# Binary cross-entropy on one core: the last full store issued from GpSimd instead of SyncE

## The chip, the core and the metric

The kernel runs on one core of a Trainium2 chip. Its time is the device time of one execution, in microseconds (us). The core has five engines that run their own instruction streams; here VectorE (DVE), ScalarE (ACT), GpSimd (POOL) and SyncE (SP) are used. Transfers between HBM and the on-chip memory SBUF are carried by 16 DMA engines. A transfer is issued by an instruction of ScalarE, GpSimd or SyncE and goes into that engine's DMA queue: in the profile q0 is GpSimd's queue, q1 SyncE's and q10 ScalarE's.

## The reference

Both inputs and the output are 8192 x 8192 float32; target holds zeros and ones.

```python
def reference(pred, target):
    eps = 1e-7
    pred = np.clip(pred, eps, 1 - eps)
    return -(target * np.log(pred) + (1 - target) * np.log(1 - pred))
```

With target 0 or 1 this is -log|pred + target - 1|, which is how the kernel computes it.

## The kernel before

The arrays are taken as flat and cut into 39 chunks, each spread over 128 partitions. Chunk 0 is 8192 elements wide in each partition, chunks 1 to 35 are 14336 wide (7168 KB in float32, or 7.34 MB), and three tail chunks follow: 6656, 6656 and 1024 wide. The last full chunk, number 35, is called z; the tail chunks 36, 37 and 38 are called a, b and c.

Two areas of SBUF hold the data. `ring_p` has three slots of 14336 float32 columns; a full chunk takes the slots in turn, and the three tail chunks lie side by side in one slot. `ring_t` has one slot of 14336 bfloat16 columns for target; the load converts float32 to bfloat16 on the way, so a target chunk reads as many bytes from HBM as a pred chunk and writes half as many into SBUF.

For each chunk there are these steps, the loop's full chunks done in halves:

- `load_p` (L70) and `load_t` (L73): load pred and target. All are issued from GpSimd, but for pred of chunk 0, which ScalarE issues.
- `clip` (L85): VectorE limits pred to [eps, 1-eps], in place.
- `merge` (L91, L94, L95): VectorE adds target - 1, in place; then ScalarE takes the absolute value and the logarithm, in place.
- `negate` (L99): VectorE multiplies by -1, in place.
- `store` (L79): the result goes from `ring_p` to HBM.

The order of the instructions on each engine is written out by hand. A trip k of the loop (k from 0 to 34) merges chunk k, loads target of k+1, negates k, clips k+1, stores k and loads pred of k+2; in this loop every store goes through GpSimd's queue. After the loop, chunk z is merged; then GpSimd issues the loads of a, b and c (pred, then target, of each). VectorE's order from there is: negate the first half of z, clip a, negate the second half of z, merge a, clip b, merge b, negate a, clip c, merge c, negate b, negate c. The stores of z, a, b and c are issued from SyncE in this order, each when its negate is done; the store of c is cut into three pieces by rows (108, 12 and 8 partitions). Dependences between engines become semaphore waits. An engine issues in program order, so an instruction that waits holds up what is behind it on the same engine.

The list `ROWS` cuts the last store, and z in the code is the number of the last full chunk.

Of the kernel before, what the change touches and what calls it, by code (L numbers as in the profile page):

```python
# [1 line left out]

# [4 lines left out]

EPS = 1e-7

WIDE = 14336  # L10
SLOTS = 3
TAIL = (6656, 6656, 1024)
ROWS = (108, 12, 8)


@with_exitstack
def kernel(
    ctx: ExitStack,
    tc: tile.TileContext,
    pred: bass.AP,  # L20
    target: bass.AP,
    out: bass.AP,
):
    nc = tc.nc
    fp32 = mybir.dt.float32
    low = mybir.dt.bfloat16
    Alu = mybir.AluOpType
    Act = mybir.ActivationFunctionType
    P = nc.NUM_PARTITIONS

    R, C = pred.shape
    total = R * C // P
    rest = total - sum(TAIL)
    n = rest // WIDE
    first = rest - n * WIDE
    assert 0 < first <= WIDE and n > 4 and sum(TAIL) <= WIDE
    spots = [(first, 0)]
    spots += [(WIDE, k % SLOTS * WIDE) for k in range(1, n + 1)]
    c = (n + 1) % SLOTS * WIDE
    for w in TAIL:  # L40
        spots.append((w, c))
        c += w
    n = len(spots)
    z = n - 1 - len(TAIL)
    starts = [sum(w for w, _ in spots[:k]) * P for k in range(n)]

    pool = ctx.enter_context(tc.tile_pool(name="rings", bufs=1))
    ring_p = pool.tile([P, SLOTS * WIDE], fp32, name="ring_p", tag="ring_p")
    ring_t = pool.tile([P, WIDE], low, name="ring_t", tag="ring_t")
    warm = pool.tile([1, 8], fp32, name="warm", tag="warm")  # L50

    def chunk(ap, k):
        flat = ap.rearrange("r c -> (r c)")
        w = spots[k][0]
        return flat[starts[k] : starts[k] + w * P].rearrange("(p w) -> p w", p=P)

    def cols(ring, k, part, c):
        w = spots[k][0]
        i, m = part
        return ring[:, c + i * w // m : c + (i + 1) * w // m]  # L60

    def p_of(k, part=(0, 1)):
        return cols(ring_p, k, part, spots[k][1])

    def t_of(k, part=(0, 1)):
        return cols(ring_t, k, part, spots[k][1] % WIDE)

    def load_p(k):
        queue = nc.scalar if k == 0 else nc.gpsimd
        queue.dma_start(out=p_of(k), in_=chunk(pred, k))  # L70

    def load_t(k):
        nc.gpsimd.dma_start(out=t_of(k), in_=chunk(target, k))  # L73

    def store(k):
        queue = nc.sync if k >= z else nc.gpsimd
        r = 0
        for rows in ROWS if k == n - 1 else (P,):
            queue.dma_start(out=chunk(out, k)[r : r + rows, :], in_=p_of(k)[r : r + rows, :])  # L79
            r += rows  # L80
        assert r == P

    def clip(k, *part):
        p = p_of(k, *part)
        nc.vector.tensor_scalar(  # L85
            out=p, in0=p, scalar1=EPS, scalar2=1 - EPS, op0=Alu.max, op1=Alu.min
        )

    def merge(k, *part):
        p, t = p_of(k, *part), t_of(k, *part)  # L90
        nc.vector.scalar_tensor_tensor(  # L91
            out=p, in0=t, scalar=1.0, in1=p, op0=Alu.subtract, op1=Alu.add
        )
        nc.scalar.activation(out=p, in_=p, func=Act.Abs)  # L94
        nc.scalar.activation(out=p, in_=p, func=Act.Ln)  # L95

    def negate(k, *part):
        p = p_of(k, *part)
        nc.vector.tensor_scalar(out=p, in0=p, scalar1=-1.0, scalar2=None, op0=Alu.mult)  # L99

    halves = (0, 2), (1, 2)
    with tc.manual_schedule():
        load_p(0)
        load_t(0)
        load_p(1)
        nc.vector.memset(warm, 1.0)  # L106
        nc.scalar.activation(out=warm, in_=warm, func=Act.Ln)  # L107
        for h in halves:
            clip(0, h)
        for k in range(z):  # L110
            for h in halves:
                merge(k, h)
            load_t(k + 1)
            for h in halves:
                negate(k, h)
            for h in halves:
                clip(k + 1, h)
            store(k)
            if k + 2 <= z:
                load_p(k + 2)  # L120
        for h in halves:
            merge(z, h)
        a, b, c = range(z + 1, n)
        for j in a, b, c:
            load_p(j)
            load_t(j)
        negate(z, halves[0])
        clip(a)
        negate(z, halves[1])
        store(z)  # L130
        merge(a)
        clip(b)
        merge(b)
        negate(a)
        store(a)
        clip(c)
        merge(c)
        negate(b)
        store(b)
        negate(c)  # L140
        store(c)


# [1 line left out]
_INS = ['pred', 'target']  # L145
_OUTS = [((8192, 8192), 'float32')]


# [23 lines left out]
```

## Time and profile before

| | |
|---|---|
| median of 3 runs | 1882.25 us (1881.54 to 1882.39) |
| the profiled execution, its own time | 1880.78 us |
| its span in the profile | 1879.0 us |
| VectorE busy | 1118.3 us, 60% of the span |
| ScalarE busy | 901.7 us, 48% |
| GpSimd busy | 282.8 us, 15% |
| read from HBM, written to HBM | 536.87 MB, 268.44 MB |
| rate counted so | 429 GB/s over the span |
| through GpSimd's queue | 652.22 MB as the DMA rows count them |
| through SyncE's queue | 14.68 MB |

The DMA rows of the profile count a transfer by one side, so a target load counts with its smaller bfloat16 size there; the HBM counts show what was read. A transfer's row gives its size and the time from issue to landing, which includes the time in which it stood in its queue behind others. A DMA share of 1 in a stretch of time means that all 16 DMA engines were busy in it. In a timeline row the first figure is the start, counted from the span's start, and the second the length; the brackets say how long the engine had stood idle before it, and what ended that. "SPq" and "POOLq" mean an instruction that issues a transfer on that engine.

### The profile page before, as it was taken

How to read it: one execution, taken by the hardware profiler on the slowest of the kernel's cores; microseconds unless marked ns; L12 is line 12 of the kernel's file. 1: busy time of each engine (PE TensorE's matmuls, PEld its weight loads, DVE VectorE, ACT ScalarE, POOL GpSimd, SP SyncE). 2: the span in 40 equal slices, each digit the busy share in tenths (PEclk: the TensorE clock that was granted, in tenths of full speed). 3: DMA queues.
4: the chain of work that ended last, by engine and by line, in shares of the span. 5: the costliest groups of instructions: out<-in, count | busy, mean ns of one | idle time of the engine just before them, and what ended most of it. 6: DMA issues, size and time to landing. Idle time of an engine off the chain costs nothing.

```text
span 1879.0 us, 697 instructions
## 1 busy us (share of the span) xinstructions
DVE 1118.3 (60%) x226; ACT 901.7 (48%) x152; POOL 282.8 (15%) x116
## 2 busy tenths in 40 slices
DVE  4675566565555665556656555566555666665563
ACT  3555444444455555554444444555555444444473
POOL 0121111111111110111111111111101111111100
DMA  9999999999999999999999999999999999999996
GB/s 329 338 375 372 370 352 366 355 352 352 359 359 355 355 371 376 374 373 359 359 358 358 352 353 361 358 354 364 375 374 374 369 353 363 355 354 354 359 363 239
DMA packets 16869, 671.14 MB, mean 357 GB/s; under 512 B 1888, under 2 KB 1888, under 8 KB 2272
## 3 DMA queue, kind: packets, MB, share of 16 engines
q0 software_dynamic: 16128, 652.22, 97.0%
q1 hardware_dynamic: 592, 14.68, 1.8%
q10 hardware_dynamic: 144, 4.19, 0.6%
q14 instruction: 5, 0.04, 0.0%
HBM read 536.87 MB, written 268.44 MB: 429 GB/s over the span
## 4 chain that ended last, share of the span: by engine, by line
DMA 64%; issue 28%; ACT 3%; DVE 2%; another core or an unknown queue 1%; POOL 0%; POOLq 0%; DVEq 0%; PEldq 0%
DMA ring_t<-in_target_dram 64%; ACT ring_p L95 2%; ACT ring_p L94 2%; DVE ring_p L91 2%; DVE ring_p L99 0%; POOL out_dram L79 0%; DVE ring_p L85 0%; POOL ring_p L70 0%; DVEq L167 0%; POOLq L73 0%; POOLq L79 0%; DVEq L91 0%; PEldq L167 0%
## 5 line engine op out<-in xcount | busy, mean ns | idle before, releaser
L94 ACT ACTIVATE ring_p<-ring_p 128x7168 f32<-128x7168 f32 (+3 forms) x75 | 451.6, 6021 | 959.1 <-DVE ring_p L91 959.1
L91 DVE SCALAR_TENSOR_TENSOR ring_p<-ring_t,ring_p 128x7168 f32<-128x7168 bf16 (+3 forms) x75 | 554.8, 7437 | 252.2 <-DMA ring_t<-in_target_dram 252.2
L99 DVE TENSOR_SCALAR ring_p<-ring_p 128x7168 f32<-128x7168 f32 (+3 forms) x75 | 285.0, 3802 | 475.0 <-ACT ring_p L95 475.0
L95 ACT ACTIVATE ring_p<-ring_p 128x7168 f32<-128x7168 f32 (+3 forms) x75 | 452.1, 6029 | 2.4
L85 DVE TENSOR_SCALAR ring_p<-ring_p 128x7168 f32<-128x7168 f32 (+3 forms) x75 | 281.9, 3799 | 20.3 <-DMA ring_p<-in_pred_dram 20.3
L79 POOL DMA_DIRECT2D out_dram<-ring_p x35 | 126.9, 3625 | 710.8 <-DVE ring_p L99 710.8
L73 POOL DMA_DIRECT2D ring_t<-in_target_dram x39 | 20.7, 532 | 801.1 <-DVE ring_p L91 800.3
L70 POOL DMA_DIRECT2D ring_p<-in_pred_dram x38 | 135.3, 3561 | 0.0
L107 ACT ACT_TABLE_LOAD x1 | 1.3, 1283 | 1.1 <-PEq L156 1.1
L106 DVE MEMSET warm<- 1x8 f32 x1 | 0.1, 65 | 0.8 <-PEq L156 0.8
L107 ACT ACTIVATE warm<-warm 1x8 f32<-1x8 f32 x1 | 0.2, 208 | 0.0
L156 POOL MEMSET const-float32-0.0<- 128x1 f32 x1 | 0.1, 100 | 0.2 <-issue 0.2
L156 POOL MEMSET const-bfloat16-1.0<- 128x1 bf16 x1 | 0.1, 102 | 0.0
L156 POOL MEMSET const-float32-1.0<- 128x1 f32 x1 | 0.1, 100 | 0.0
L156 POOL MEMSET const-uint8-127<- 128x1 uint8 x1 | 0.1, 99 | 0.0
## 6 DMA issues: line engine op xcount, KB each, us to landing
ring_p<-in_pred_dram POOLq DMA_DIRECT2D x35, 7168.0 KB, 44.4
out_dram<-ring_p POOLq DMA_DIRECT2D x34, 7168.0 KB, 31.0
ring_t<-in_target_dram POOLq DMA_DIRECT2D x35, 3584.0 KB, 35.2
out_dram<-ring_p SPq DMA_DIRECT2D x1, 7168.0 KB, 28.9
ring_p<-in_pred_dram POOLq DMA_DIRECT2D x2, 3328.0 KB, 34.7
out_dram<-ring_p SPq DMA_DIRECT2D x2, 3328.0 KB, 9.6
ring_p<-in_pred_dram ACTq DMA_DIRECT2D x1, 4096.0 KB, 19.6
out_dram<-ring_p POOLq DMA_DIRECT2D x1, 4096.0 KB, 21.2
```

The lines of the kernel that those rows point to most:

```text
L70: queue.dma_start(out=p_of(k), in_=chunk(pred, k))
L73: nc.gpsimd.dma_start(out=t_of(k), in_=chunk(target, k))
L79: queue.dma_start(out=chunk(out, k)[r : r + rows, :], in_=p_of(k)[r : r + rows, :])
L85: nc.vector.tensor_scalar(out=p, in0=p, scalar1=EPS, scalar2=1 - EPS, op0=Alu.max, op1=Alu.min)
L91: nc.vector.scalar_tensor_tensor(out=p, in0=t, scalar=1.0, in1=p, op0=Alu.subtract, op1=Alu.add)
L94: nc.scalar.activation(out=p, in_=p, func=Act.Abs)
L95: nc.scalar.activation(out=p, in_=p, func=Act.Ln)
L99: nc.vector.tensor_scalar(out=p, in0=p, scalar1=-1.0, scalar2=None, op0=Alu.mult)
L106: nc.vector.memset(warm, 1.0)
L107: nc.scalar.activation(out=warm, in_=warm, func=Act.Ln)
L156: nc = _bacc.Bacc("TRN2", target_bir_lowering=False, num_devices=1)
```

## The change

The store of chunk z, 128 x 14336 float32, is issued from GpSimd instead of SyncE. On GpSimd it stands behind the last loads (pred and target of a, b and c), as the last transfer that this engine issues. The stores of a, b and c stay on SyncE. Nothing else is changed: the same bytes are moved, and the other engines' instructions are the same in the same order.

```diff
     def store(k):
-        queue = nc.sync if k >= z else nc.gpsimd
+        queue = nc.sync if k > z else nc.gpsimd
         r = 0
         for rows in ROWS if k == n - 1 else (P,):
             queue.dma_start(out=chunk(out, k)[r : r + rows, :], in_=p_of(k)[r : r + rows, :])
```

## The prediction

> Below, z is the last full chunk and a, b, c are the three tail chunks; p, t and s stand for a chunk's load of pred, its load of target and its store. "s_z" is the store that moves. A change of 0.2%, 3.8 us here, is about the least that a measurement of this kernel can tell from none.
>
> **What bounds the kernel now.** I read the page's DMA row first, then the rows of every engine in the tail, then each tail transfer's row, then the DMA share in stretches of 2 us. On the page:
>
> ```profile
> DVE 1118.3 (60%) x226; ACT 901.7 (48%) x152; POOL 282.8 (15%) x116
> DMA  9999999999999999999999999999999999999996
> q0 software_dynamic: 16128, 652.22, 97.0%
> q1 hardware_dynamic: 592, 14.68, 1.8%
> ```
>
> No engine is near full, and the transfers run without a break until the last slice of 47 us. So whatever moves the end keeps the DMA engines filled near the end, or moves fewer bytes. The timeline of the tail (start, length, engine):
>
> ```profile
> 1814.18 0.39 SPq L79 DMA_DIRECT2D out_dram<-ring_p  x1
> ...
> 1821.07 3.62 DVE L85 TENSOR_SCALAR ring_p<-ring_p 128x6656 f32<-128x6656 f32 x1
> 1843.69 7.09 DVE L91 SCALAR_TENSOR_TENSOR ring_p<-ring_t,ring_p 128x6656 f32<-128x6656 bf16 x1 [19.00 <-DMA ring_t<-in_target_dram]
> 1850.70 3.62 DVE L99 TENSOR_SCALAR ring_p<-ring_p 128x6656 f32<-128x6656 f32 x1
> ...
> 1866.04 0.33 SPq L79 DMA_DIRECT2D out_dram<-ring_p  x1
> ```
>
> VectorE has clipped b by 1824.69 and then stands 19.00 us for t_b; only then come merge(b), negate(a), s_a and all that follows. And the stretches (DMA share and GB/s are the last two figures):
>
> ```profile
> 1845.00:1847.00 2.00, 2.00 (x1) 0.00 (x0) 0.00 (x0) 1.00 0.03 6
> ...
> 1853.00:1855.00 2.00, 1.97 (x3) 2.00 (x1) 0.00 (x0) 1.00 0.00 0
> 1855.00:1857.00 2.00, 1.18 (x1) 1.97 (x2) 0.00 (x0) 1.00 1.01 426
> ...
> 1861.00:1863.00 2.00, 0.62 (x1) 2.00 (x2) 0.00 (x0) 1.00 0.99 426
> 1863.00:1865.00 2.00, 2.00 (x1) 1.35 (x2) 0.00 (x0) 1.00 0.00 0
> 1865.00:1867.00 2.00, 1.61 (x2) 0.00 (x0) 0.00 (x0) 1.00 0.47 200
> ```
>
> The DMA engines are empty from 1846 to 1855 and again from 1863 to 1866: there the end is lost. The cause is in the landing times (the last figure is us from issue to landing; t_b, issued at 1793.36, and then s_z, issued at 1814.18):
>
> ```profile
> ring_t<-in_target_dram POOLq DMA_DIRECT2D x1, 1664.0 KB, 50.2
> ...
> out_dram<-ring_p SPq DMA_DIRECT2D x1, 7168.0 KB, 28.9
> ```
>
> Landings, as issue plus that time: s of chunk z-1 1763.71+31.0 = 1794.7; p_a 1767.33+35.3 = 1802.6; t_a 1785.83+24.7 = 1810.5; p_b 1786.35+34.2 = 1820.6; t_b 1843.6; p_c 1793.88+51.0 = 1844.9; t_c 1794.40+51.7 = 1846.1; s_z 1843.1. t of chunk z had landed at 1742.62+35.19 = 1777.8. While GpSimd's queue is alone its transfers land strictly in order, spaced by size: 16.9 us for a full store, 7.9 for a 6656-wide load, of pred or of target. From 1814.18 that spacing breaks: p_b takes 10.1 after t_a, t_b 23.0 after p_b. s_z on SyncE's queue took its share ahead of loads that were issued 20 us before it.
>
> **The change, part by part.**
>
> *Removed: s_z on SP.* One issue of 0.39 us at 1814.18. SP issues nothing else until s_a, so the issue itself frees nothing. What goes is its competition with p_b, t_b, p_c, t_c. Alone in their queue they land at the spacing above: p_b 1810.5+7.9 = 1818.4, t_b 1826.3, p_c 1826.3+1.2 (1024/6656 of 7.9) = 1827.5, t_c 1828.7.
>
> *Added: s_z on GpSimd.* The built program has it behind t_c, its only live wait the negates of z, which end at 1810.26+3.89 = 1814.15. GpSimd starts about 0.3 us after a release (t_a at 1785.83, behind a merge that ended at 1777.91+7.62 = 1785.53). Its issue costs 0.53 by t_a's row, beside a merge, or 3.63 by the rows of all earlier stores:
>
> ```profile
> 1763.33 3.89 DVE L85 TENSOR_SCALAR ring_p<-ring_p 128x7168 f32<-128x7168 f32 x1
> 1763.71 3.63 POOL L79 DMA_DIRECT2D out_dram<-ring_p  x1 [20.56 <-DVE ring_p L99]
> ```
>
> That store ends 0.1 us behind the clip beside it. At 1814 the neighbour is merge(a), as with t_a, so I take 0.53: done at 1815.0; by the other end 1818.1; were it held through merge(a) and clip(b), 1824.7+3.6 = 1828.3. All three lie before 1828.7, when the queue ahead of it runs dry, so the cost is zero. If that cover were gone it would be 0.5 to 3.6 us on s_z. A gain is excluded: s_z can't pass t_c. Nothing is queued behind it on GpSimd but the program's end.
>
> The Trainium skill ("SBUF — State Buffer", section "SBUF: two separate sides") speaks against the move: descriptors of a DMA issued from GpSimd can't be written while VectorE runs an operation in its two-port mode, and those from SP are free of that. The 3.63 beside a clip and the 0.53 beside a merge agree; by that rule, too, the sum stays as it is, since merge(a) is the neighbour.
>
> *Moved: the chain behind t_b.* merge(b) can start at 1826.4 instead of 1843.69: 17.3 earlier, later than clip(b)'s end at 1824.69 and not needing ScalarE. After it the chain is what it was: negate(a) needs ScalarE's Ln of a, 1826.97+5.75 = 1832.7, and merge(b) ends at 1833.5, so negate(a) ends at 1837.1; ScalarE's b starts with merge(b)'s end. s_a is issued at 1854.35-17.3 = 1837.1, s_b at 1866.04-17.3 = 1848.7, s_c's three pieces from 1849.3. SP's waits ahead of s_a are for that negate and for transfers that ended long before.
>
> *Moved: when the bytes flow.* The queue's work up to s_z is the same bytes as before, and the engines were kept filled: from t_a's landing, 7.9+7.9+1.2+1.2+16.9 = 35.1 us of work gives 1845.6; measured, in the order of before, 1846.1. I keep 1846.1. s_a joins at 1837.1+0.65 (in before, issue 1854.35, flow from 1855.0) and adds 8.0 us (1855.0 to 1863.0): with s_z it runs until 1854.1, without a gap. s_b is there from 1849.3, so it too flows without a gap, until 1862.1. In before it landed at 1866.04+10.0 = 1876.0. So the end moves by 1876.0-1862.1 = **13.9 us**. What follows it (the pieces of c on the same queue, the end of the program: 1879.0-1876.0 = 3.0) stays. s_z lands between 1846.1 and 1854.1, ahead of the end, so the wait of the program's end for it costs nothing.
>
> The unknown is the rate of two stores side by side, 1837.8 to 1854.1, which before does not show. Bounds: 434 GB/s as in the loop (a trip of 50.7 us reads or writes three times 7.34 MB, target counted as read), and 329 GB/s, the page's first slice, where ScalarE's and GpSimd's queues load together: 16.3 us of work would take 21.5, costing 5.2. A gain over 434 is bounded by the chain: s_b can't be issued before 1848.7, so at most 17.3 instead of 13.9. I take 434, the nearest row being the mix of s_z with loads, which reached 1846.1 against 1845.6 worked out.
>
> The profiled execution took 1880.78 (span 1879.0 plus 1.8), 1.5 under the median. By its own time the forecast is 1880.8-13.9 = 1866.9; against the median of 1882.25, **1868.4**.
>
> **The rivals.**
>
> *1. Queues don't matter (about 1882).* s_z could interleave with the loads from whichever queue it comes; then t_b lands at 1843.6 again and nothing moves: 1882.3. For it: the DMA engines were equally full in either phase. Against it: in the loop, stores and loads of GpSimd's queue land in order at a fixed spacing, 16.9 and 7.9, and only the store from SP broke it. The Trainium skill ("DMA: Bandwidth & Descriptors", section "Issuing engines are not separate DMA queues") says that DMAs interleave whichever engine started them; by that rule the change would give 1882.3. The same page, section "Queues, rings and completion order", has each DMA engine go round between queues but consume one queue's entries in order; t_b's 50.2 us agrees with this one. Chance 0.04.
>
> *2. Slower: two stores side by side slow each other.* Place: 1837.8 to 1854.1, s_z on GpSimd's queue and s_a on SP's, both reading SBUF and writing HBM. It decides once the 16.3 us of work take 13.9 more, that is below 434*16.3/30.2 = 234 GB/s. At 200 GB/s it is 35.4 us, 19.1 more: 1887.5. For it: no row shows two stores at once. Against it: single stores flow at 426, and the store beside loads cost half a microsecond in all. Chance 0.03.
>
> *3. A milder form of 2,* between 329 and 234 GB/s: 5.2 to 13.9 back, 1873.6 to 1882; 1877 in its middle. Chance 0.05.
>
> *4. The chain sets the end.* If s_z and s_a were moved faster than 434, s_b would find the engines free at 1848.7 and all moves by 17.3: 1865.0. Against it: nothing in the tail flows above 434 for long. Chance 0.08.
>
> *5. The change doesn't take.* In the built program SP has one issue less and GpSimd one more, behind t_c, and no other engine differs; I give it nothing.
>
> **How the numbers follow.** Forecast 0.80, rivals 0.04, 0.03, 0.05, 0.08. The likeliest case is 1868.4. The range takes in rival 4 at its low end with a microsecond for spread between executions, 1864, and the 329 GB/s bound at the high end, 1873.6; outside lie rivals 1 to 3, 0.12 in all, and a little of the rest. Faster by over 0.2% (under 1878.5): forecast, 4, and 0.03 of 3's middle and lower part, less a little for a step unseen: 0.91. Same: 0.05. Slower: 0.04.
>
> **What would show it.** t_b's landing near 33 us after issue instead of 50.2, the 19.00 us stall before merge(b) down to about 1.7; s_z's issue near 0.5 us on GpSimd, and its landing 32 to 40 us after; s_a's and s_b's landings longer than 9.3 and 10.0 (about 17 and 13), as they now queue; no empty stretch of DMA between 1814 and the end; span near 1865. The forecast is wrong if t_b still lands late (rival 1), or if s_z with s_a show a share near one at well under 400 GB/s (2 and 3).

## The result, and the profile after

The changed kernel took 1867.99 us (median of 6 runs, 1866.10 to 1868.84) against 1881.59 before (6 runs, 1881.44 to 1882.39): 13.6 us less, ratio 0.9925 with a 95% interval of 0.9912 to 0.9937. In a later set of runs the ratio was 0.9924 (0.9912 to 0.9937). The forecast was 13.9 us less.

The page of the changed kernel, engine row, DMA row and queues:

```profile
DVE 1118.2 (60%) x226; ACT 901.7 (48%) x152; POOL 283.3 (15%) x117
DMA  9999999999999999999999999999999999999998
q0 software_dynamic: 16272, 659.56, 98.5%
q1 hardware_dynamic: 448, 7.34, 0.9%
```

The engines do what they did; 7.34 MB went from SP's queue (q1) to GpSimd's (q0), and the last slice is fuller. The loop of this execution ran 1.7 us later than in the profile of before (t of chunk z landed at 1744.40+35.15 = 1779.55, there at 1777.81), so times of the two tails are compared after taking 1.7 off. From that landing to the end of the span before took 101.2 us and after 87.6: the 13.6 us of the runs lie wholly in the tail. A second profile of the changed kernel, from the later set, has 86.7 here, so what is read from a single profile is good to about 1 us.

The tail's timeline in the changed kernel:

```profile
1816.18 0.54 POOL L79 DMA_DIRECT2D out_dram<-ring_p  x1 [19.50 <-DVE ring_p L99]
...
1828.07 7.09 DVE L91 SCALAR_TENSOR_TENSOR ring_p<-ring_t,ring_p 128x6656 f32<-128x6656 bf16 x1 [1.65 <-DMA ring_t<-in_target_dram]
...
1850.42 0.35 SPq L79 DMA_DIRECT2D out_dram<-ring_p  x1
```

VectorE's wait for t_b has gone from 19.00 us to 1.65, s_b is issued at 1850.42 (1848.7 on the clock of before) instead of 1866.04, and s_z costs GpSimd 0.54 us. The tail's transfers, with the time from issue to landing at the end: t_b, s_z, s_a, s_b.

```profile
ring_t<-in_target_dram POOLq DMA_DIRECT2D x1, 1664.0 KB, 32.9
...
out_dram<-ring_p POOLq DMA_DIRECT2D x1, 7168.0 KB, 34.2
...
out_dram<-ring_p SPq DMA_DIRECT2D x1, 3328.0 KB, 16.5
...
out_dram<-ring_p SPq DMA_DIRECT2D x1, 3328.0 KB, 13.6
```

t_b lands 17.3 us sooner after its issue; each of the stores takes longer than before, because it now queues behind or beside other transfers. In stretches of 2 us (DMA share and GB/s are the last two figures):

```profile
1841.00:1843.00 2.00, 0.00 (x0) 2.00 (x1) 0.00 (x0) 1.00 0.60 259
1843.00:1845.00 2.00, 0.00 (x0) 2.00 (x1) 0.00 (x0) 1.00 1.04 450
...
1859.00:1861.00 2.00, 0.00 (x0) 0.00 (x0) 0.00 (x0) 1.00 0.72 239
1861.00:1863.00 2.00, 0.00 (x0) 0.00 (x0) 0.00 (x0) 1.00 0.30 97
1863.00:1865.00 2.00, 0.00 (x0) 0.00 (x0) 0.00 (x0) 1.00 0.07 27
```

The two empty stretches are gone: from 1816 to 1859 the lowest share is the 0.60 shown, beside stretches above 1. From 1859 on the share fades slowly. Such a fading stood before ahead of the first empty stretch (shares of 0.78, 0.25 and 0.03 from 1841 to 1847); now it stands at the end. A share of 0.07 is about one DMA engine of 16: the others have by then all but finished s_b and c, and the end waits for one.

### The profile page after: what moved, and what is told of

The parts are those of the page before. It is cut to its first block, busy times and chain, and to the rows that moved or that the text cites. A ratio compares the mean times of both kernels' runs of the same rounds, so it can differ in the third digit from the quotient of the medians.

```text
span 1867.1 us, 695 instructions
## 1 busy us (share of the span) xinstructions
DVE 1118.2 (60%) x226; ACT 901.7 (48%) x152; POOL 283.3 (15%) x117
## 3 DMA queue, kind: packets, MB, share of 16 engines
q1 hardware_dynamic: 448, 7.34, 0.9%
## 4 chain that ended last, share of the span: by engine, by line
DMA 67%; issue 28%; DVE 2%; ACT 2%; POOL 0%; POOLq 0%; DVEq 0%; PEldq 0%
DMA ring_t<-in_target_dram 67%; DVE ring_p L91 2%; ACT ring_p L95 1%; ACT ring_p L94 1%; DVE ring_p L99 0%; POOL out_dram L79 0%; POOL ring_p L70 0%; DVEq L167 0%; POOLq L73 0%; POOLq L79 0%; DVEq L91 0%; PEldq L167 0%
```

## The experiments

The question was which property of the move brought the gain: the place of s_z in the order of the bytes, or GpSimd's queue as such; and then what sets the end now. Each set of runs had its own runs of the kernel before, whose medians were 1882.95, 1882.52 and 1881.67; differences are taken within a set.

**SP's queue, held back.** s_z stays on SP, behind a 128-byte copy that has to wait for t_b.

```diff
         negate(z, halves[1])
+        nc.sync.dma_start(out=gate, in_=t_of(b)[0:1, 0:64])
         store(z)
```

> s_z stays on SP, but SP first issues a 128-byte copy that reads t_b, so it waits until t_b has landed; then s_z follows. Nothing is left out. Theory (s_z hurts by taking its share of the DMA engines ahead of the loads; from which queue it then comes is of no account): t_b lands about 33 us after its issue, as in the changed kernel, s_z is issued at about 1827 and flows at once, no DMA engine that matters runs dry, and the time is that of the changed kernel, 1868, give or take 1.5. Rival (GpSimd's queue as such carries the store better): t_b early, but the end no better than 1878.

Measured: 1867.20 us (1866.92 to 1867.84), ratio 0.9917 (0.9903 to 0.9932), 15.7 under before in its set. The timeline of this kernel's SP and VectorE, and its row of s_z:

```profile
1826.85 0.56 SPq L131 DMA_DIRECT2D gate<-ring_t  x1
1826.87 7.09 DVE L92 SCALAR_TENSOR_TENSOR ring_p<-ring_t,ring_p 128x6656 f32<-128x6656 bf16 x1 [1.63 <-DMA ring_t<-in_target_dram]
```
```profile
out_dram<-ring_p SPq DMA_DIRECT2D x1, 7168.0 KB, 18.7
```

The whole gain is had with s_z on SP, once it no longer runs beside the loads: GpSimd's queue as such is not the cause.

**A third queue, not held back.** s_z from ScalarE.

```diff
-        queue = nc.sync if k >= z else nc.gpsimd
+        queue = nc.scalar if k == z else nc.sync if k > z else nc.gpsimd
```

> s_z is issued from ScalarE at the same moment, a third queue. Theory: it takes its share ahead of the loads as from SP; t_b's landing is again near 50 us, s_z's near 29, and the time is that of before, 1882 within 1 us. Rival (it was SP's queue in particular, by s_z standing ahead of s_a on it): a gain of several us.

Measured: 1881.41 us (1880.51 to 1883.77), ratio 0.9994 (0.9984 to 1.0003). VectorE's wait and t_b's row in this kernel:

```profile
1844.66 7.09 DVE L91 SCALAR_TENSOR_TENSOR ring_p<-ring_t,ring_p 128x6656 f32<-128x6656 bf16 x1 [18.88 <-DMA ring_t<-in_target_dram]
```
```profile
ring_t<-in_target_dram POOLq DMA_DIRECT2D x1, 1664.0 KB, 50.1
```

A store from another queue than the loads' delays them, from ScalarE's (18.88 us of wait) as from SP's (19.00).

**Half and half.** The first half of the columns from SP, the second from GpSimd.

```diff
-        store(z)
+        for h, queue in zip(halves, (nc.sync, nc.gpsimd)):
+            i = h[0] * WIDE // 2
+            queue.dma_start(out=chunk(out, z)[:, i : i + WIDE // 2], in_=p_of(z, h))
```

> s_z cut by columns: the first half from SP, the second from GpSimd behind the loads. Theory: 8.45 us of work on SP's queue share the engines evenly with p_b and t_b, so t_b lands 8.4 later than in the changed kernel, about 41.3 us after its issue; s_b is issued 8.4 later, but the engines are busy for about 5 of these, so the end comes 3.6 later than in the changed kernel: about 1871.6. If the chain of engines set the end in the changed kernel: 8.4 later, 1876.4. If the gain were in proportion to the bytes moved to GpSimd: 1874.8.

Measured: 1874.00 us (1872.27 to 1877.82), ratio 0.9956 (0.9941 to 0.9971), 9.0 under before by the medians. The interval, 5.5 to 11.1 under before, holds the theory's 10.0 as well as the proportional 6.8 and lies just clear of 5.2, so the time alone doesn't decide between the first two. The profile says more: t_b landed 41.9 us after its issue where 41.3 was expected.

```profile
ring_t<-in_target_dram POOLq DMA_DIRECT2D x1, 1664.0 KB, 41.9
```

I had put the first half's issue at 1814; it was issued at 1804.19, as soon as its own negate was done. On the clock of before t_b landed at 1835.3, 9.0 later than in the changed kernel, and the span ended 5.2 later. So 3.8 us of the chain's delay were covered (2.9 against the second profile of the changed kernel), where I had said 5.

**GpSimd's queue, in the wrong place.** s_z from GpSimd ahead of the loads of b and c.

```diff
-        for j in a, b, c:
+        load_p(a)
+        load_t(a)
+        negate(z, halves[0])
+        clip(a)
+        negate(z, halves[1])
+        store(z)
+        for j in b, c:
             load_p(j)
             load_t(j)
-        negate(z, halves[0])
-        clip(a)
-        negate(z, halves[1])
-        store(z)
```

> s_z on GpSimd, but issued ahead of p_b, t_b, p_c, t_c instead of behind them. Theory (the order of the bytes decides, not the queue): GpSimd waits until 1814 for s_z, its queue runs empty from 1810.5 for some 5 us, then s_z takes 16.9, p_b 7.9 and t_b 7.9, so that t_b lands at about 1848.3, 4.7 later than before: the time is about 1886.3. Rival (GpSimd's queue as such is better for this store): still under 1880.

Measured: 1888.32 us (1887.11 to 1895.21), ratio 1.0035 (1.0022 to 1.0048): slower than before by 5.4 at the medians, 6.6 by the ratio, against 4.7 expected. In the profile:

```profile
1844.53 3.63 DVE L85 TENSOR_SCALAR ring_p<-ring_p 128x6656 f32<-128x6656 f32 x1 [21.17 <-DMA ring_p<-in_pred_dram]
1852.44 7.09 DVE L91 SCALAR_TENSOR_TENSOR ring_p<-ring_t,ring_p 128x6656 f32<-128x6656 bf16 x1 [4.28 <-DMA ring_t<-in_target_dram]
```
```profile
out_dram<-ring_p POOLq DMA_DIRECT2D x1, 7168.0 KB, 19.9
```

Same queue, other place: the gain turns into a loss. What I missed is that s_z, issued into an empty queue, landed 19.9 us after its issue where I had counted 16.9 of flow and about 1 of start. Of the change as made this cost is hidden, since the queue still holds loads when s_z arrives.

**More work in the chain ahead of s_b.** The absolute value of chunk b taken twice or three times, in the changed kernel and, twice, in the one before; the result is the same.

```diff
-        nc.scalar.activation(out=p, in_=p, func=Act.Abs)
+        for _ in range(2 if k == n - 2 else 1):
+            nc.scalar.activation(out=p, in_=p, func=Act.Abs)
```

> The changed kernel with the absolute value of chunk b taken twice: 5.75 us more in the chain of engines ahead of s_b, the result unchanged. Theory (in the changed kernel the DMA engines set the end, and one that lags is ready for s_b only about 4.8 us after s_b's issue): s_b is issued 5.75 later, the end comes about 1 us later, 1869. Rival (the chain of engines sets the end): 5.75 later, 1873.7.

> The kernel before with the same second absolute value of chunk b. The DMA engines are empty when s_b is issued there, so the chain sets the end: 5.75 later, 1887.4. If the DMA engines had set the end: under 1884.

> The changed kernel with the absolute value of chunk b taken three times: 11.5 us more ahead of s_b. Theory: beyond the slack of 4.8 the chain sets the end, 6.7 later than the changed kernel: 1874.7, and 5.75 later than with two. Rival (the chain sets the end from the start): 11.5 later, 1879.5.

Measured in one set: before with one more 1888.11 us (ratio 1.0027, 1.0018 to 1.0036), 5.6 over before; the changed kernel with one more 1870.71 (ratio 0.9935, 0.9920 to 0.9950) and with two more 1876.10 (0.9965, 0.9951 to 0.9979). So one more operation costs 5.6 before, and the second one in the changed kernel 5.4, both about the 5.75 of its length; the first one in the changed kernel costs about 2 (11.8 under before in its set, where the unaltered change is 13.6 under). Differences of medians between sets are uncertain by 2 to 3 us; the profiles, counted from the landing of t of chunk z, give 1.9 and 7.7 for one and two over the first profile of the changed kernel. By these the slack is 3.8 us (5.75-1.9, and 11.5-7.7). Both figures lean on that one profile, and against the second one the slack is 2.9. So it lies at some 3 to 4 us: below it the DMA engines set the end, above it the chain does. I had expected 4.8.

**All tail stores from GpSimd.**

```diff
-        queue = nc.sync if k > z else nc.gpsimd
+        queue = nc.gpsimd
```

> All four tail stores are issued from GpSimd. Theory (the loads ahead of s_z are what counts; two stores side by side on two queues cost nothing): within 1.5 us of the changed kernel, 1868. If s_a and s_z on two queues slow each other: a further gain of 2 us or more. The straggling DMA engine at the end stays either way.

Measured: 1867.44 us (1867.03 to 1868.41), ratio 0.9916 (0.9901 to 0.9931). Whether s_a runs beside s_z from another queue or behind it in the same makes no difference that these runs can tell.

**What the last store's shape does now.** Four kernels in one set: the changed kernel again; c's store in one piece; two tail chunks of 7168 in place of the three, the same elements in all (the instructions of chunk c go with it and are not shown); and the latter with all stores from GpSimd.

```diff
-ROWS = (108, 12, 8)
+ROWS = (128,)
```
```diff
-TAIL = (6656, 6656, 1024)
+TAIL = (7168, 7168)
-ROWS = (108, 12, 8)
+ROWS = (128,)
```

> The changed kernel again, as the mark for the three beside it: 13.6 us under before, ratio 0.9925.

> The changed kernel with s_c as one store of 128 rows. Theory (one lagging DMA engine sets the end, and in the last stretch it carries 11 of the 128 rows of c at 0.155 us each): with 8 rows it ends 0.5 us earlier, which is at the edge of what can be measured. Rival (the cut into 108, 12 and 8 rows still helps at the end): 0.5 to 1.5 us later.

> The changed kernel with two tail chunks of 7168 and no third; the same bytes in all. Theory (the DMA engines set the end, so a small last store is of no more use): s_b is issued about 4 us later, which the slack of 4 to 5 still covers, the rows of c no longer stand behind it: within 1.5 us of the changed kernel, rather below. Rival (the chain sets the end): 2 to 4 us later.

> As the kernel with two tail chunks of 7168, and all stores from GpSimd. Theory: as that one within 1 us. If GpSimd's queue ends the program later or sooner than SP's, it shows here.

Measured: 1867.53 (1866.96 to 1868.78), 1866.41 (1866.37 to 1866.48), 1866.34 (1866.21 to 1869.14) and 1871.75 (1871.25 to 1871.78). One piece is 1.1 under the changed kernel of its set, the way that was expected (0.5), but the ratios to before, 0.9917 (0.9903 to 0.9930) and 0.9924 (0.9912 to 0.9937), overlap; the kernel without c isn't told apart from the changed kernel either. So the small last store, cut in three, no longer earns anything, and a version that is surely better than the change was not found. The fourth was a miss: 5.4 over the third by the medians, and its fastest run (1871.25) is slower than the third's slowest (1869.14). Its transfers were done in time:

```profile
out_dram<-ring_p POOLq DMA_DIRECT2D x1, 3584.0 KB, 10.2
```
```profile
1865.00:1867.00 2.00, 0.00 (x0) 0.00 (x0) 0.00 (x0) 1.00 0.00 0
```

s_b, issued at 1854.04, landed at 1864.2, and the span ended at 1870.0, 5.8 later; in the third kernel, where s_a and s_b come from SP, s_b's landing and the end lie under 2 us apart. It is a wait at the program's end and no transfer. The trace shows for what: the DRAIN instruction behind GpSimd's last issue starts at 1854.02, takes 14.84 us (the longest of the row's three, in ns below) and so ends at 1868.86, 4.7 us after s_b's landing; the last waits of the other engines end right behind it, at 1869.0.

```profile
L163 POOLq DRAIN  x3: 46/235/14837, 1854.0 to 1869.7; - x3
```

In twelve of the other thirteen profiles this DRAIN also ends 4.6 to 4.7 us after the last transfer of GpSimd's queue has landed, but SP's later stores hide it: in the changed kernel it ends at 1855.0, 9 us before s_b lands. In the kernel with chunk c and all four tail stores on GpSimd it ends only 0.5 us after the last landing; why it is short there, the runs don't settle.

## Why the prediction was right, point by point

- *The cause* (s_z takes its share ahead of loads issued earlier): shown by three runs together. From SP held back, the gain stays (15.7); from ScalarE not held back, it is nil (ratio 0.9994); from GpSimd ahead of the loads, it is a loss (ratio 1.0035).
- *t_b's landing*: 32.9 after its issue as forecast, by the spacing of 7.9 per 6656-wide load. The stall of 1.65 follows the forecast 1.7.
- *s_z's issue on GpSimd*: 0.54, beside merge(a), as taken from t_a's row; the other end of that bound, 3.63, was not seen.
- *The chain moves by 17.3*: s_a is issued at 1838.73-1.7 = 1837.0 (forecast 1837.1), s_b at 1848.7 (1848.7).
- *The end moves by less, 13.9, because the DMA engines are still busy*: the span's tail shrank by 13.6. s_b landed at 1850.42+13.6 = 1864.0, 1862.3 on the clock of before (forecast 1862.1), and 3.1 us followed it (3.0). Runs and forecast agree here to 0.3 us, closer than two profiles of the changed kernel do (0.9), so the last tenths are luck.
- *Two stores side by side at 434 GB/s*, the unknown of the sum: s_a, issued at 1838.73, landed at 1855.2 or 1853.5 on the old clock, where 1854.1 was forecast, so there was no loss; rivals 2 and 3 are out. With all stores in one queue the time is the same. The lower bound of 329 GB/s was no rate of two queues: the page counts a target load by its bfloat16 size, and on that count the loop's own slices show 352 to 376 where the sum has 434. The forecast didn't use it; the upper end of the range did.
- *Rival 1* (queues don't matter) is out by t_b's row. The Trainium skill's sentence that transfers interleave whichever engine started them ("DMA: Bandwidth & Descriptors", section "Issuing engines are not separate DMA queues") is true of this kernel across queues, and that is the harm: s_z from SP and from ScalarE interleaved with the loads (50.2 and 50.1 us for t_b). Within GpSimd's queue it did not hold: t_b took 32.9 with s_z behind it.
- *Rival 4* (the chain sets the end) is out for the change as made, but nearer than its working had it: the slack is some 3 to 4 us by the profiles, where the sum had 4.8 (1854.1 less 1849.3).
- *The program's end costs nothing for s_z*: so it was, because s_z landed at 1850.4, long before the end. GpSimd's DRAIN ended 4.7 us after that landing, which the working had not counted; a store that lands last on GpSimd's queue can cost them, as the fourth kernel above shows.
- *What the working had wrong, without harm to the sum*: it treated the 16 DMA engines as one that finishes at one moment. They don't; the next but one section has the numbers. The sum came out because the figure that it started from, 1846.1, was itself the landing on the last engine.

## What to carry to other kernels

A store that is ready while the last loads are still queued should not go out on a queue of its own when those loads lead to the end: here that cost 17 us on a load and 13.6 on the end. Put it behind the loads in their queue, or hold it until they have landed; both gave the same time. To size such a change, follow the chain and the bytes separately and take the later of the two: the chain moved by 17.3 and the DMA engines gave back only 13.6.

## What the runs showed of the hardware

The DMA engines drift apart while their queue never runs dry. Every transfer over all 128 partitions leaves 16 marks of completion in the trace, which I take as one from each DMA engine. In the profile of before, the marks of one GpSimd transfer lie 0.7 us apart at the start, 2.9 at 420 us, and 3.25 from 730 us to the tail; in that of the changed kernel 4.1 at 420 us and 4.8 at the tail. The middle of them lies only 0.4 to 0.5 behind the first, so a few engines lag, and they stay behind. Once the queue runs dry, the marks close up: 0.16 us apart for s_a of before, which flowed after 9 empty us, and 0.5 for the transfers behind the empty stretch of the kernel with s_z ahead of the loads. In the changed kernel nothing runs dry, so s_b was done on its first engine at about 1859.6 and on its last at 1864.0: this is the fading in its last stretches. What makes an engine fall behind, the traces don't show.

The lag is also most of what differs between the loops of one execution and the next. In all fourteen profiles, whose loops are the same, the first mark of t of chunk z lies between 1774.4 and 1775.5, and the last one, for which VectorE waits, anywhere from 1777.8 to 1781.2. Of the 1.7 us by which the loop of the changed kernel's profile ran later than that of before, 1.6 are a wider lag (4.8 against 3.2).

The kernel with s_z held back on SP shows that only the last engine counts. Its DMA engines stood mostly idle in the stretch before t_b had wholly landed, where those of the changed kernel were full (shares of 1.27 and 1.18 in the two stretches around its landing of t_b):

```profile
1825.00:1827.00 2.00, 0.37 (x2) 2.00 (x1) 0.00 (x0) 1.00 0.36 101
...
1859.00:1861.00 2.00, 0.00 (x0) 0.00 (x0) 0.00 (x0) 1.00 1.04 426
1861.00:1863.00 2.00, 0.00 (x0) 0.00 (x0) 0.00 (x0) 1.00 0.56 180
```

And yet the end was the same: the engines that paused had been ahead, and their store then flowed in step with the laggard's (s_z's marks lie 0.3 us apart there, 6.8 in the changed kernel), at a full share until 1861 where the changed kernel's was fading from 1859.
